# Ordering the mixers' threads by an account of the engines, in place of written latencies

## The chip, the cores and the metric

One core of a Trainium2 chip runs one program. The metric is the device time of one execution in microseconds (us). TensorE (PE) does the matrix products, VectorE (DVE), ScalarE (ACT) and GpSimd (POOL) the rest; SyncE (SP) issues nearly all weight loads. Every engine works through its own queue in program order, so the order in which the program is written down (emitted) is the order in which each engine takes its work up.

## The reference

Two transformer blocks in float32 on 256 tokens of width 1024: three mixers, each followed by a mixture of 32 experts (MoE).

```python
x = first_block(x, c, ...)    # two layers: even mixer, MoE 0, odd mixer, MoE 1
return second_block(x, ...)   # one layer: second mixer, MoE 2, final norm
# even:   o = concat(sliding-window attention, gated linear attention) @ w_out
# odd:    o = block attention (one block of 256 here, 8 heads) @ w_out
# second: o = (gate_nsa * (nsa @ w1) + gate_hg * (hgrn2 @ w2)) @ w_out
# MoE:    two of the 32 experts for each token, silu(t@w1)*(t@w3) @ w2
```

## The kernel before

**Weights.** All weights, some 700 MB, stream once through `ring`, 19 slots of 1 MB. `plan` fills a list in order of use; `pump` (L183 to L195) issues the next load when a slot is free, and `done`/`release` free slots as the program is emitted. SP waits at each load until the slot's last reader has finished.

**Stages.** Even mixer, MoE 0, odd mixer, MoE 1, second mixer, MoE 2. In a MoE each pair of experts takes 12 loads of 1 MB, and PE uses them as they land.

**A mixer** multiplies the activations by its weights in `slab` (from L468): for each 2 x 512 piece of weights `prep` splits the float32 weights in two parts (cast on ACT L461, subtractions on DVE L462 and POOL L463) and PE runs three products. Beside this stream of weight products run smaller threads, all Python generators: in the even mixer `gla` (gated linear attention) and `swa`, `swa_tile` (the window attention, scores at L856, softmax to L871); in the odd mixer `transposed` and eight `head`s (softmax at L1054 to L1063); in the second mixer `nsa_prep`, `nsa_attn` (scores L1269, exponentials L1275, normalisation L1287) and `hgrn` (levels, each ending at L1375). `mix` puts modulation products (`mod`, weights ada_w, the tile condz) between the stream's steps: eight in the even mixer's slabs and two in its first output half, six in the odd mixer, none in the second.

**What sets the order.** `weave` (L213) takes the first thread in its list that is ready, the stream being last, and emits its next step; when none is ready it goes to the one that is ready first. A thread says with `yield (a, b)` that the step took PE a us and that its next step is ready b us after; with `yield (key, ...)` that it waits for flags; `flag(key, lat)` sets a flag to now + lat. All of a, b and lat are written numbers. Those that matter below: each of the four score steps of a `swa_tile` ends with `yield (0.22*nb, 13.3)`; a softmax in `nsa_attn` has 4.0 after the exponentials and 2.0 after the normalisation, and 0.8 after each two score groups; a level of `hgrn` has 7.0 and then 1.0; in the odd mixer's stream the step that reads the gate's rows and issues 15 small loads on ACT's queue (`router` L1614 to L1622 and `second_setup` L1156) ends with `yield (3.8, 0.3)`. The stream waits for the flags of the window attention ("oa") before its first output half in the even mixer, and for "nsa" before its last input slabs in the second.

Of the kernel before, what the change touches and what calls it, by code (L numbers as in the profile page):

```python
# [10 lines left out]
FR = mybir.dt.float32r  # L11
# [108 lines left out]
    return c  # L120


class Net:
    def __init__(self, tc, ctx, A, out):
        self.tc, self.nc, self.A, self.out = tc, tc.nc, A, out
        nc = self.nc
        pool = lambda name, bufs=1, **k: ctx.enter_context(tc.tile_pool(name=name, bufs=bufs, **k))
        c = self.cp = pool("const")
        self.ring = pool("ring", RING)
        self.ps = pool("ps", 8, space=PSUM)  # L130
        self.dp = pool("scratch", space=DRAM)
        self.flip = 0
        self.queue, self.live, self.chunks = [], {}, {}
        self.free, self.reserve, self.wanted = RING, 0, []
        self.now, self.flags = 0.0, {}
        self.more, self.mine, self.extra = [], set(), None
        km = c.tile([P, 476], FT, name="km")
        self.km = km
        self.ident = km[:, 0:128]
        self.ltri = km[:, 128:256]  # L140
        self.ones = km[:, 256:384]
        self.iota = km[:, 384:448]
        self.selc = km[:, 448:464]
        self.tie4 = km[:, 464:468]
        self.tie8 = km[:, 468:476]
        self.x = c.tile([P, NT, D], FT, name="x")
        self.fb = ExitStack()
        self.fp = self.fb.enter_context(tc.tile_pool(name="first", bufs=1, side="right"))
        self.rb = ExitStack()
        self.rp = self.rb.enter_context(tc.tile_pool(name="rows", bufs=1, side="right"))  # L150
        self.ga = self.fp.tile([P, D], FT, name="ga")
        self.ssq = c.tile([P, NT, 4], FT, name="ssq")
        self.mhalf = c.tile([P, 16], FT, name="mhalf")
        nc.gpsimd.memset(self.mhalf, -0.5)
# [52 lines left out]
        self.release(len(keys) - n, reserve)  # L207


    def flag(self, key, lat=0.0):  # L210
        self.flags[key] = self.now + lat

    def weave(self, *gens):  # L213
        th = [[g, self.now, ()] for g in gens]
        while th:
            best = None
            for x in th:
                if any(k not in self.flags for k in x[2]):
                    continue
                r = max([x[1]] + [self.flags[k] for k in x[2]])  # L220
                if r <= self.now + 1e-9:
                    best = (r, x)
                    break
                if best is None or r < best[0]:
                    best = (r, x)
            assert best, [x[2] for x in th]
            r, x = best
            self.now = max(self.now, r)
            try:
                y = next(x[0])  # L230
            except StopIteration:
                th.remove(x)
                continue
            if isinstance(y[0], (int, float)):
                self.now += y[0]
                x[1], x[2] = self.now + y[1], ()
            else:
                x[1], x[2] = self.now, y
        self.flags = {}
# [1777 lines left out]
def body(tc, A, out):  # L2017
    with ExitStack() as ctx:
        ctx.enter_context(tc.manual_schedule())
        n = Net(tc, ctx, A, out)  # L2020
        n.plan_even()
        n.plan_moe(0)
        n.plan_odd()
        n.plan_moe(1)
        n.plan_second()
        n.plan_moe(2)

        n.reserve = 6
        n.even(lambda: n.norm_coeffs(0, 7, 3, 4))
        n.moe(0, n.ev[6], lambda: n.gate_coeffs(0, 5), lambda: n.norm_coeffs(1, 6, 0, 1), 8)  # L2030
        bp = ctx.enter_context(ExitStack())
        n.bias1 = bp.enter_context(tc.tile_pool(name="bias", bufs=1, side="right")).tile([P, 8, T], FT, name="bias1")
        pb = ctx.enter_context(ExitStack())
        n.pre = pb.enter_context(tc.tile_pool(name="pre", bufs=1))
        n.odd(lambda: n.norm_coeffs(1, 7, 3, 4))
        bp.close()
        n.rb.close()
        n.moe(1, n.od[5], lambda: n.gate_coeffs(1, 5), lambda: n.norm_coeffs(1, 8), 14)
        n.fb.close()
        n.second(lambda: n.norm_coeffs(1, 9))  # L2040
        pb.close()
        n.extra = ctx.enter_context(tc.tile_pool(name="extra", bufs=2, side="right"))
        n.more = [n.extra] * 2
        n.moe(2, (), lambda: None, lambda: None, 0)


INPUTS = [
# [23 lines left out]
```

## Time and profile before

| | |
|---|---|
| median of 3 runs (lowest to highest) | 2085.38 us (2081.81 to 2085.57) |
| the profiled execution | 2082.4 us, of which the span of instructions is 2080.6 us |
| PE busy | 1885.0 us, 91% |
| DVE, ACT, POOL busy | 859.2, 431.3, 309.6 us |
| DMA | 725.30 MB, mean 349 GB/s, 421 GB/s in the MoE stages |

The stages, from the span's start: even mixer to about 216 us, MoE 0 to 695, odd mixer to 857, MoE 1 to 1337, second mixer to 1609, MoE 2 to the end. Where the DMA engines are fully busy the loads set the pace; elsewhere one asks what PE waits for.

### The profile page before, as it was taken

To read this page: it belongs to the slowest core of one execution; us is meant where nothing else is said; L and a number is where in the kernel's file an instruction comes from. 1 tells how busy PE (TensorE), PEld (TensorE's weight loads), DVE (VectorE), ACT (ScalarE), POOL (GpSimd) and SP (SyncE) were. 2 spreads that over 40 slices of the span, in tenths; PEclk is the share of its full clock that TensorE was granted. 3 is DMA by queue.
4 is the path that set the end of the run, shared out by engine and by line. 5 is a ranking of instruction groups with operands and counts; after the bars stand their busy time and mean duration, and the time that the engine had idled before them with its cause. 6 is when DMAs were issued, how large, how long until landed. Compare 5 with 4: busy or idle time off the path is not lost. (4 is left out here: it accounts for less than half of the span.)

```text
span 2080.6 us, 25139 instructions
## 1 busy us (share of the span) xinstructions
PE 1885.0 (91%) x10032; PEld 1039.9 (50%) x10032; DVE 859.2 (41%) x1601; ACT 431.3 (21%) x790; POOL 309.6 (15%) x245
## 2 busy tenths in 40 slices
PE   5898899899999889899999999998899999899997
PEld 3656444434444657544343444586788444344443
DVE  3665433323332657633223332367666332222223
ACT  1423211111010333311010111244543111001111
POOL 1331000000000424100000000143443000000000
PEclk8997999999999999999999999899999999999999
DMA  9696999999999966799999999931357999999997
GB/s 322 258 304 236 363 422 422 420 421 421 421 421 406 343 214 247 303 391 421 421 420 421 421 421 421 337 111 41 123 191 270 373 421 421 420 421 421 421 421 270
DMA packets 157542, 725.30 MB, mean 349 GB/s; under 512 B 25305, under 2 KB 43087, under 8 KB 85225
## 3 DMA queue, kind: packets, MB, share of 16 engines
q1 hardware_dynamic: 139216, 716.84, 86.0%
q10 hardware_dynamic: 18201, 6.76, 1.3%
q8 instruction: 82, 1.34, 0.3%
q14 instruction: 43, 0.35, 0.0%
HBM read 722.48 MB, written 1.07 MB: 348 GB/s over the span
## 5 line engine op out<-in xcount | busy, mean ns | idle before, releaser
L258 PE MATMUL ps<-slot,xg 128*64 128x512 f32 x2952 | 680.9, 598 | 0.0
L258 PEld LDWEIGHTS ps<-slot,xg 128*64 128x64 f32 x2952 | 231.0, 138 | 408.7 <-issue 391.7
L258 PE MATMUL ps<-slot,ht 128*64 128x512 f32 (+1 forms) x1592 | 344.8, 574 | 67.6 <-issue 62.9
L258 PE MATMUL ps<-slot 128*128 128x256 f32 (+8 forms) x2230 | 369.9, 326 | 14.0 <-DVE slot L462 9.6
L258 PEld LDWEIGHTS ps<-slot 128*128 128x128 f32 (+3 forms) x2230 | 300.4, 186 | 74.0 <-issue 16.0
L258 PEld LDWEIGHTS ps<-slot,ht 128*64 128x64 f32 x1592 | 130.3, 138 | 257.0 <-issue 244.3
L1908 DVE TENSOR_TENSOR x<-x,ps 128x512 f32<-128x512 f32 x180 | 115.2, 681 | 246.1 <-PE ps L258 246.1
L1882 POOL TENSOR_TENSOR yl<-sg,yh 128x512 fp32r<-128x512 f32 (+1 forms) x68 | 82.4, 1212 | 870.8 <-ACT yh L1881 870.8
L463 POOL TENSOR_TENSOR slot<-slot 128x512 fp32r<-128x512 f32 (+2 forms) x108 | 163.7, 1533 | 282.4 <-ACT slot L461 265.6
L1861 DVE SCALAR_TENSOR_TENSOR hh<-sg,ws,ps 128x512 f32<-128x512 f32 x48 | 53.4, 1113 | 316.5 <-PE ps L258 203.4
L1881 ACT CAST yh<-sg 128x512 fp32r<-128x512 f32 (+1 forms) x68 | 40.3, 593 | 466.1 <-DVE sg L1880 466.1
L462 DVE TENSOR_TENSOR slot<-slot 128x512 fp32r<-128x512 f32 (+2 forms) x108 | 107.4, 1008 | 55.6 <-ACT slot L461 55.1
L1880 DVE TENSOR_TENSOR sg<-ps,ga 128x512 f32<-128x512 f32 (+1 forms) x68 | 44.9, 660 | 178.7 <-PE ps L258 178.7
L258 PEld LDWEIGHTS ps<-u,slot 128*128 128x128 f32 x864 | 104.4, 192 | 23.4 <-issue 17.0
L461 ACT CAST slot<-slot 128x1024 fp32r<-128x1024 f32 (+2 forms) x108 | 106.5, 1020 | 44.8 <-PE ps L258 24.7
L258 PE MATMUL ps<-u,slot 128*128 128x256 f32 (+1 forms) x864 | 109.7, 285 | 3.5 <-DVEq L1743 3.5
L1857 ACT ACTIVATE sg<-ps 128x512 f32<-128x512 f32 x48 | 28.7, 598 | 297.9 <-PE ps L258 297.9
L258 PE MATMUL ps<-yh,pg 128*128 128x512 f32 (+1 forms) x204 | 87.2, 429 | 0.7 <-ACT yh L1881 0.7
L258 PE MATMUL ps<-yl,pg 128*128 128x512 f32 (+1 forms) x204 | 78.5, 387 | 4.3 <-POOL yl L1882 4.0
L399 ACT ACTIVATE xg<-ps,cf 128x256 f32<-128x256 f32 (+1 forms) x72 | 38.9, 540 | 168.0 <-PE ps L258 168.0
L1933 POOL TENSOR_TENSOR slot<-x,rows 128x512 f32<-128x512 f32 x2 | 2.5, 1270 | 463.0 <-DVE x L1929 463.0
L1884 ACT CAST yh<-ps 128x512 fp32r<-128x512 f32 (+1 forms) x34 | 19.0, 560 | 222.7 <-PE ps L258 222.6
(333 smaller groups left out, 1569.3 us busy)
## 6 DMA issues: line engine op xcount, KB each, us to landing
slot<-moe_w SPq DMA_DIRECT2D x376, 1024.0 KB, 17.7
slot<-w_gate SPq DMA_DIRECT2D x59, 1024.0 KB, 19.7
slot<-w_down SPq DMA_DIRECT2D x55, 1024.0 KB, 18.5
slot<-w_up SPq DMA_DIRECT2D x54, 1024.0 KB, 18.8
slot<-ada_w SPq DMA_DIRECT2D x48, 1024.0 KB, 8.8
slot<-w_in SPq DMA_DIRECT2D x20, 1024.0 KB, 5.7
slot<-odd_w_in SPq DMA_DIRECT2D x12, 1024.0 KB, 16.8
more<-w_up SPq DMA_DIRECT2D x10, 1024.0 KB, 16.1
```

The costliest lines, as they stand in the source:

```text
L258: self.nc.tensor.matmul(out, lhsT=lhsT, rhs=rhs, start=start, stop=stop)
L399: self.nc.scalar.activation(out, p, AF.Identity, scale=a, bias=nb[:, k:k + 1])
L461: nc.scalar.copy(wh, src)
L462: nc.vector.tensor_sub(wl[:, 0], src[:, 0], wh[:, 0].bitcast(FT))
L463: nc.gpsimd.tensor_sub(wl[:, 1], src[:, 1], wh[:, 1].bitcast(FT))
L1857: nc.scalar.activation(sg, ps, AF.Silu)
L1861: nc.vector.scalar_tensor_tensor(ha.rearrange("s k p -> s p k"), st["sg", p].rearrange("s (p k) -> s p k", k=4), st["ws", p], ps.rearrange ...
L1880: nc.vector.tensor_mul(y, ps, self.ga[:, sl])
L1881: nc.scalar.copy(yh, y)
L1882: nc.gpsimd.tensor_sub(yl, y, yh.bitcast(FT))
L1884: nc.scalar.copy(yh, ps)
L1908: nc.vector.tensor_add(self.x[:, t, sl], self.x[:, t, sl], ps)
```

## The change

The written numbers stay in the code but are hardly used. An object `Queues` is told of every instruction as the program is built. It keeps a clock for each engine (its queue's end), the times at which pieces of tiles are written and read, and one clock for all loads (400 bytes a ns, 2.0 us to land; an issue takes its engine 0.4 us). `now` is its clock of PE. A step whose b is 0 leaves the thread ready at once, as before; a step whose b is not 0 makes it ready when the last result of that step, by the account, is there. A flag is set to the end of its step's results so far. Results of loads issued by ACT count in this; those of SP don't. No instruction is added to the program or taken out.

```diff
+class Queues:
+    def cost(self, kind, engine, ins, outs):
+        n = max([o[5] for o in outs], default=1)
+        if engine == "PE":
+            if kind != "InstMatmult":
+                return 0.05
+            one = len(ins) and ins[0][6] == FR
+            width = outs[0][2] - outs[0][1]
+            t = n * 0.000417 * (1 if one else 2 if n <= 128 else 4) + 0.013
+            return t * (0.55 if width <= 64 else 1.0)
+        base, slope = {"Activation": (0.2, 0.00082), "DVE": (0.16, 0.00104), "Pool": (0.4, 0.0023)}.get(engine, (0.05, 0.0))
+        return base + slope * n
+
+    def __call__(self, inst):
...
+        start = max(self.clock.get(engine, 0.0), self.clock.get("PE", 0.0) if dma else 0.0)
...
+        if dma:
+            size = sum(128 * o[5] * 4 for o in outs)
+            self.clock[engine] = start + 0.4
+            end = max(start, self.clock.get("fetch", 0.0)) + size / 4e5
+            self.clock["fetch"] = end
+            end += 2.0
+        else:
+            end = start + self.cost(kind, engine, ins, outs)
+            self.clock[engine] = end
+            if outs:
+                end += 0.06
...
+        if outs and not (dma and engine == "SP"):
+            self.end, self.touched = max(self.end, end), True
...
+    @property
+    def now(self):
+        return self.queues.clock.get("PE", 0.0)
+
     def flag(self, key, lat=0.0):
-        self.flags[key] = self.now + lat
+        self.flags[key] = max(self.now, self.queues.end) if self.queues.touched else self.now
...
             r, x = best
-            self.now = max(self.now, r)
+            q.clock["PE"] = max(self.now, r)
+            q.end, q.touched = 0.0, False
...
             if isinstance(y[0], (int, float)):
-                self.now += y[0]
-                x[1], x[2] = self.now + y[1], ()
+                x[2] = ()
+                x[1] = self.now if not y[1] else max(self.now, q.end) if q.touched else self.now + y[1]
```

## Rows read from the trace of the kernel before

**Rows 1.** The page: busy us, share and instructions; DMA busy in 40 slices.
```profile
PE 1885.0 (91%) x10032; PEld 1039.9 (50%) x10032; DVE 859.2 (41%) x1601; ACT 431.3 (21%) x790; POOL 309.6 (15%) x245
DMA  9696999999999966799999999931357999999997
```
**Rows 2.** Windows: length, busy PE, PEld, DVE, ACT, POOL, granted clock, DMA share, GB/s.
```profile
45.00:151.70 106.70, 97.76 (x581) 65.90 (x581) 70.76 (x125) 37.05 (x52) 40.24 (x32) 0.97 0.84 292
151.70:176.10 24.40, 12.77 (x50) 7.43 (x48) 14.23 (x46) 12.00 (x41) 1.55 (x1) 0.65 0.76 283
240.00:695.00 455.00, 418.35 (x2046) 188.00 (x2044) 140.02 (x220) 53.87 (x102) 43.25 (x37) 0.99 1.01 414
752.00:776.00 24.00, 17.66 (x93) 10.95 (x92) 6.74 (x17) 6.97 (x14) 4.72 (x3) 0.86 0.73 240
1392.00:1488.00 96.00, 81.55 (x606) 66.03 (x606) 69.35 (x178) 47.58 (x110) 30.92 (x22) 0.93 0.24 77
1488.00:1609.00 121.00, 119.40 (x924) 109.13 (x923) 80.51 (x116) 57.88 (x80) 52.16 (x34) 0.99 0.57 204
1650.00:2040.00 390.00, 361.33 (x1752) 158.14 (x1749) 110.65 (x188) 36.89 (x68) 0.00 (x0) 1.00 1.01 421
```
**Rows 3.** Waits of PE, 240 to 690: us in total, times, longest.
```profile
PE ps L258 <- issue: 21.0, 14, 1.6
```
**Rows 4.** Waits of PE in the even mixer, 45 to 216.
```profile
PE ps L268 <- DVE slot L871: 6.6, 1, 6.6
...
PE ps L268 <- DVE slot L798: 3.9, 1, 3.9
```
**Rows 5.** Timeline, even mixer: start us, us, instruction, [idle before <- releaser].
```profile
108.63 0.92 PE L258 MATMUL ps<-kT,qT 64*128 64x256 f32 x8
...
151.04 0.70 PE L258 MATMUL ps<-kT,qT 64*128 64x256 f32 x4
...
164.49 2.22 PE L268 MATMUL ps<-km,slot 128*128 128x128 f32 x8 [6.57 <-DVE slot L871]
```
**Rows 6.** The same on DVE: eight normalisations of one window-attention tile.
```profile
163.99 2.19 DVE L871 TENSOR_SCALAR slot<-slot,den 128x256 f32<-128x256 f32 x8
```
**Rows 7.** Timeline of ACT's queue in the odd mixer, first and last of 15 issues.
```profile
754.17 0.58 ACTq L1619 DMA_DIRECT2D wr<-moe_w_group  x1
...
761.87 0.35 ACTq L1156 DMA_DIRECT2D ll<-hg_lb_logits  x1
762.26 0.92 ACT L254 CAST slot<-ps 128x256 fp32r<-128x256 f32 x3 [7.51 <-DMA k_cmp<-k_cmp]
```
**Rows 8.** Timeline of PE at the same place.
```profile
759.47 1.92 PE L258 MATMUL ps<-slot,condz 128*32 128x512 f32 x16
761.32 3.06 PE L258 MATMUL ps<-slot 128*128 128x512 f32 x12
770.67 0.88 PE L268 MATMUL ps<-km,sc 128*128 128x128 f32 x3 [6.29 <-DVE sc L1063]
```
**Rows 9.** Waits of PE in the second mixer, 1337 to 1609.
```profile
PE ps L268 <- DVE slot L1287: 13.3, 9, 2.5
```
**Rows 10.** Timeline of PE, second mixer: two score steps, the last slab before "nsa".
```profile
1436.34 1.13 PE L258 MATMUL ps<-kd,qT 64*128 64x256 f32 x8
...
1438.99 1.14 PE L258 MATMUL ps<-kd,qT 64*128 64x256 f32 x8
...
1465.05 8.34 PE L258 MATMUL ps<-slot 128*128 128x512 f32 x36
1475.85 0.33 PE L268 MATMUL ps<-km,slot 128*128 128x128 f32 x1 [2.46 <-DVE slot L1287]
```
**Rows 11.** Timeline of DVE: the last reduction of the first of these score steps.
```profile
1438.33 0.42 DVE L1269 CUSTOM_DVE_ANT_0 slot<-ps,k_causal 128x256 f32<-128x256 f32 x1
```
**Rows 12.** Two lines of the kernel: count, ns min/median/max, first to last start.
```profile
L1287 DVE TENSOR_SCALAR slot<-slot,den x32: 273/340/1347, 1405.8 to 1480.1; 128x128 f32<-128x128 f32 x16, 128x256 f32<-128x256 f32 x16
...
L1375 DVE COPY_PREDICATED slot<-lvm,ps x7: 724/736/754, 1433.3 to 1516.8; 128x512 f32<-128x512 uint32 x7
```

More of the change, by code (lines that the diff above doesn't have):

```diff
@@ L120, in host_constants, with __init__, part @@
     return c
+class Queues:
+    def __init__(self):
+        self.clock, self.tiles, self.end, self.touched = {}, {}, 0.0, False
+    @staticmethod
+    def part(arg):
+        ap = getattr(arg, "bass_ap", None)
+        if ap is None or not hasattr(ap, "tensor"):
+            return None
+        try:
+            dims, off = [(int(a), int(b)) for a, b in ap.ap], int(ap.offset)
+        except (TypeError, ValueError):
+            return None
+        step = max(1, dims[0][0])
+        lo = off % step
+        hi = lo + sum(abs(a) * (b - 1) for a, b in dims[1:]) + 1
+        n = 1
+        for a, b in dims[1:]:
+            n *= b
+        return ap.tensor.name, off // step, off // step + dims[0][1], lo, hi, n, arg.dtype
+    def cost(self, kind, engine, ins, outs):
[10 more added lines that the diff above has]
+    def __call__(self, inst):
+        engine = str(inst.engine).split(".")[-1]
+        kind = type(inst).__name__
+        outs = [p for p in map(self.part, inst.outs) if p]
+        ins = [p for p in map(self.part, inst.ins) if p]
+        dma = "DMA" in kind
+        start = max(self.clock.get(engine, 0.0), self.clock.get("PE", 0.0) if dma else 0.0)
+        for parts, write in ((ins, False), (outs, True)):
+            for p in parts:
+                for q in self.tiles.get(p[0], ()):
+                    if (write or q[5]) and q[0] < p[2] and p[1] < q[1] and q[2] < p[4] and p[3] < q[3]:
+                        start = max(start, q[4] + (0.07 if q[6] != engine else 0.0))
+        if dma:
[9 more added lines that the diff above has]
+                end += 0.06
+        for parts, write in ((ins, False), (outs, True)):
+            for p in parts:
+                seen = self.tiles.setdefault(p[0], [])
+                seen.append((p[1], p[2], p[3], p[4], end, write, engine))
+                if len(seen) > 96:
+                    del seen[:32]
+        if outs and not (dma and engine == "SP"):
+            self.end, self.touched = max(self.end, end), True
@@ L134, in __init__ @@
         self.free, self.reserve, self.wanted = RING, 0, []
-        self.now, self.flags = 0.0, {}
+        self.flags, self.queues = {}, Queues()
+        nc.push_inst_callback(self.queues)
         self.more, self.mine, self.extra = [], set(), None
@@ L207, in done @@
         self.release(len(keys) - n, reserve)
+    @property
+    def now(self):
+        return self.queues.clock.get("PE", 0.0)
     def flag(self, key, lat=0.0):
-        self.flags[key] = self.now + lat
+        self.flags[key] = max(self.now, self.queues.end) if self.queues.touched else self.now
     def weave(self, *gens):
         th = [[g, self.now, ()] for g in gens]
+        q = self.queues
         while th:
@@ L2044, in body @@
         n.moe(2, (), lambda: None, lambda: None, 0)
+        n.nc.pop_inst_callback()
 INPUTS = [
```

## The prediction

> **What bounds the kernel now.** I read the page first: PE is busy 91% of the span, and the slices of DMA alternate between long full stretches and dips [rows 1]. The windows say which stretch has which limit [rows 2]. In the MoE stages the DMA share is 1.01 while PE still has room (418.35 of 455.00 us in MoE 0, 361.33 of 390.00 in MoE 2), and the waits of PE there are short ones that no engine ends, 14 of up to 1.6 us [rows 3]: the loads set the pace. In the mixers it is the other way round: DMA share 0.84, 0.76, 0.73, 0.24 in four stretches, PE nearly full where nothing goes wrong (119.40 of 121.00 us at the end of the second mixer) and short of work elsewhere [rows 2]. So a MoE ends a fixed time after its loads have become continuous, and that moment hangs on when the mixer before it gives up its slots. A microsecond taken from the PE path of a mixer moves the loads of the following MoE by about a microsecond and comes out at the end; idle time inside a MoE is not touched by the change at all.
>
> The whole prize is therefore PE's idle time inside the three mixers. There are three places, and they differ in what could fill them.
>
> **Even mixer, the tail.** From 151.70 to 176.10 PE is busy for 12.77 of 24.40 us, at a mean granted clock of 0.65 [rows 2]. The waits are for the window attention and the gated attention: 6.6 us for the normalisation at L871, 3.9 us for L798 [rows 4]. The stream has emitted all it may and stands at the "oa" flags. Why is the window attention so late? Its score steps: one at 108.63, PE work 0.92 us for both tiles, the last ones only from 151.04 on [rows 5]. They are spaced by the written 13.3 us each. Under the account a score step is ready again when its own reductions are done: by the constants in the diff about 0.9 us of PE and 0.43 us for each of two reductions of 256 columns, say 3 us with what stands in DVE's queue and one stream step. Four steps then take some 12 us in place of over 42, so the attention ends some 30 us earlier in the queue, near 146, before the stream reaches its wait. The tail then holds only its work. What is that at the full clock? The mean of 0.65 between the levels 1.2 and 2.4 GHz means 17.1 us at the lower; 11.6 us of the 24.4 were idle; the busy part at full clock is then between 6.4 us (all 12.77 at the lower level) and 10.0 us (all idle time at the lower level); I take 8. Gain at most 24.4 - 8 = 16.4 us. Cover: the attention's 8 us move among slab steps that PE has to do anyway, and DVE was busy 70.76 of 106.70 us there [rows 2], so it has room for the moved 14.23 us, but not without queueing. The change also brings an error of its own: eight modulation products are priced 8 x (512 x 0.000417 x 4 + 0.013) x 0.55 = 3.8 us by the account, while the trace has 1.92 us [rows 8]. After each of them the account's PE clock is 1.9 us ahead and a thread's next step can come that much too early. Ten of them: between 0 and 19 us; since a loss needs a thread becoming ready just there, I take 3. Even mixer: **-13 us** (from -16.4 to +3: nothing gained and that loss kept).
>
> **Odd mixer, the loads issued by ACT.** ACT issues 15 small loads between 754.17 and 762.22 and computes nothing [rows 7]; the head whose transposes are at PE's front waits 6.29 us at 770.67 [rows 8]. The account does see the issues (15 x 0.4 = 6 us, against 8.05 in the trace), so a head's step after them is put back. But the stream's step ends with b = 0.3, and its new meaning is "when the last result is there", and landed loads of ACT count: 6 us of issues, some 1.5 us of copies and 2.0 us to land hold the stream for about 9.5 us in place of 0.3. What stood in front of the head's transposes from 759.47 on, one modulation and 12 products (1.92 + 3.06 = 5.0 us), goes behind it. The new wait is then 6.3 + 5.0 less what the head gains where no weight split stands before its normalisation on DVE. That gain I bound by 0 and 5.0 us and take 4. With 2 us from other early transposes in this mixer I put the odd mixer at **0 us** (-6.3, the wait gone, to +5.0). Behind the held stream stand its weight splits on ACT and DVE and so the slots for SP; the heads gain from that, the loads lose as much as the stream.
>
> **Second mixer, the softmaxes.** From 1392 to 1488 PE is idle for 14.45 us [rows 2], 13.3 us of it at transposes that wait for the normalisation at L1287 [rows 9]. The written 4.0 + 2.0 us are too short. The account puts the transposes later, and slab steps go before them. But that alone wins nothing: the stream's last slab before "nsa" ends at 1473.4, before the last of the attention's waits at 1475.85 [rows 10]. Had the slabs filled the earlier gaps, they would have run out sooner, and PE would have waited at the end. Filling pays only with work that would otherwise come after 1488, and `hgrn` has that: its seven levels end from 1433.3 to 1516.8, 83.5/6 = 13.9 us apart [rows 12], where the account will bring a level every 6 to 7 us (one POOL subtraction of 1.6 us, an exponential of 1.0, four DVE operations of 0.7, by its constants). I credit 8 of the 14.45 us. Against it: a score step is now followed only after its reductions. The second one of rows 10 came 2.65 us after the first; the last reduction of the first ended at 1438.75 [rows 11], 2.41 us after its start, so with a slab step's grain the next comes 0 to 1.5 us later than now. Four such places: 0 to 6, I take 3. And DVE, which carries the chain, gets `hgrn`'s levels ahead of it: I take 2 here; the case where it is much more is a rival. Second mixer: 8 - 3 - 2, **-3 us** (-14.45 to +28).
>
> What the account prices wrongly on DVE can be seen in one row: the 32 normalisations took 273 ns at the least and 1347 at the most [rows 12], and eight of them 2.19 us where POOL is quiet [rows 6]; the account gives each of 256 columns 426 ns always, 3.4 us for eight. The Trainium skill, SBUF — State Buffer, section "SBUF: two separate sides", says that such a DVE operation and one of GpSimd exclude each other for the whole of an instruction. The maximum in this trace agrees with that. By that rule the levels' POOL subtractions, brought closer together, speak against this change; a whole subtraction by the account's own price (1.6 us) in each of the four softmaxes would take 6 us off the gain.
>
> The sum: -13 + 0 - 3 = -16 us. Against the profiled execution's own 2082.4 us (span 2080.6 and 1.8 around it) that is 2066.4; this execution lies 3.0 us under the median of the runs shown, so on the median's scale it is 2085.4 - 16 = **2069.4 us**. Instructions, weight bytes and MoE stages cost nothing more or less.
>
> **Rivals.**
>
> *The gap only moves* (2085). The even tail closes, but what is moved forward crowds DVE in 105 to 150, and the odd and second mixer lose 13 us between them (the bounds +5.0 and +28 leave room). Speaks for it: each of the three mixers has a stretch where PE waits for a chain and not for its own queue. Against: the even tail is plain want of work, and the four mean DMA shares show slots and loads waiting, not full.
>
> *The levels overtake the attention* (2100, slower). In the second mixer `hgrn` runs at its natural pace. Two levels fall into each of the four softmaxes, and their DVE work goes into the queue ahead of the normalisations: 2 x 4 x 0.74 = 5.9 us, and two normalisations each at 1.35 in place of 0.27 us, 2.1 us [rows 12]: 8 us x 4 = 32. PE has 4 us more of `hgrn`'s products to fill with. So "nsa" comes late and the mixer loses 28 us; with the even mixer's gain 2085.4 + 28 - 13 = 2100. It decides from the point where the four softmaxes lose over 4 + 13 + 4 = 21 us together, 5 us each. For it: DVE was busy already 69.35 of 96.00 us. Against: that leaves 26.65 us of room, and `nsa_attn` goes before `hgrn` when both are ready.
>
> *Everything closes* (2048). The even tail by 16.4, the odd wait by 6.3, the second mixer's 14.45 filled with `hgrn`: 2085.4 - 37.
>
> That the change doesn't alter the order is hardly possible: 13.3 against some 3 us is too far apart. If it were so the time would be 2085, and it is counted with the moved gap.
>
> **How the numbers follow.** Forecast 0.50 with its own range of 2058 to 2081 (even -13 by 4, second -3 by 6, odd 0 by 4, added roughly); moved gap 0.17; levels overtake, or another loss of that size in an order that nobody has looked at, 0.24; all closes 0.09. For 8 in 10 the range reaches from 2048 to 2102. A measurement of this kernel can tell some 0.2%, 4.2 us, from no change: faster is 0.47 of the forecast and 0.09, 0.56; same is the rest of the forecast and most of the moved gap, 0.17; slower 0.27.
>
> **What the changed profile would show.** Even: the last kT,qT products of the window attention before 130, no idle PE of over 2 us ahead of the first output half, and granted clock near 1.0 there; if "oa" still ends a wait of several us, the first step is wrong. MoE: stretches of the same length, each beginning earlier; if the mixer ends earlier and the MoE does not, the loads didn't move and my main assumption falls. Odd: a wait of 6 to 9 us after ACT's 15 issues; gone means I misread the held stream. Second: L1375 closer than 10 us apart, fewer waits for L1287; if instead the stretch from the first L1287 to the first Sigmoid slab after "nsa" grows by over 10 us, the levels overtook. The prediction is wrong altogether if PE finds new waits of tens of us, above all for loads or weight splits that the account believes to be there.

## The result, and the profile after

The change makes the kernel slower: 2111.82 us median (2109.05 to 2120.6, 4 runs) against 2085.48 (2081.81 to 2087.46, 4 runs) beside it, a ratio of 1.0136 [1.0102 to 1.0169]. I had forecast 2069.4 in a range of 2048 to 2102; the time lies above the range. The profiled execution of the kernel after is its slowest, 2120.6 us (span 2118.8), 8.8 over its median; so sizes of the loss are taken below from ratios, and the traces show the places. The page after, the lines that answer to [rows 1]:

```profile
PE 1902.8 (90%) x10032; PEld 1049.3 (50%) x10032; DVE 851.4 (40%) x1601; ACT 432.5 (20%) x790; POOL 308.0 (15%) x245
...
DMA  8668999999999847799999999931256899999997
```

The number of instructions is the same on every engine. The windows of the kernel after (length, busy PE, PEld, DVE, ACT, POOL, granted clock, DMA share, GB/s), to be held against [rows 2]; the last two are the softmax attention of the second mixer and what follows it:

```profile
45.00:151.70 106.70, 86.92 (x489) 57.93 (x490) 61.57 (x138) 40.77 (x83) 28.98 (x23) 0.88 0.65 234
151.70:188.50 36.80, 32.11 (x175) 19.60 (x174) 20.75 (x36) 9.27 (x13) 14.28 (x11) 0.95 1.03 361
240.00:695.00 455.00, 419.58 (x2048) 186.39 (x2046) 137.94 (x217) 49.53 (x90) 40.49 (x33) 0.99 1.01 413
...
1414.80:1524.60 109.80, 84.28 (x645) 67.62 (x646) 73.53 (x187) 53.73 (x114) 31.63 (x23) 0.88 0.19 65
1524.60:1657.90 133.30, 128.18 (x917) 114.67 (x915) 78.37 (x140) 53.75 (x79) 50.07 (x32) 0.99 0.61 223
```

MoE 0 is as it was. The even mixer's hole has moved: the first stretch, nearly full before (97.76 of 106.70 us), now has 19.8 us without work, and the tail is filled but for one wait. Stage by stage (a mixer ends, and a MoE begins, with the routing's first product of `top`; a mixer begins with its first product of `sel,x`; read from the timelines of PE):

| us | even | MoE 0 | odd | MoE 1 | second | MoE 2 |
|---|---|---|---|---|---|---|
| before | 227.7 | 467.4 | 173.9 | 468.1 | 284.3 | 459.1 |
| after | 234.1 | 468.4 | 187.9 | 470.2 | 297.3 | 460.8 |
| of it PE at the lower clock, before and after | 41.0, 47.8 | 10.2, 10.2 | 17.1, 31.2 | 10.2, 16.5 | 27.3, 37.7 | 9.3, 13.7 |

All three mixers are longer. The even one varies between executions in one and the same order: in the twelve traces that have it in the written order it takes 222.3 to 227.7 us, and in the other trace with the order of the kernel after (`e1_even`) 231.3.

**Even mixer.** PE's waits after, from 45 us to the routing (us in total, times, longest), in place of [rows 4]:

```profile
PE ps L334 <- issue: 8.0, 1, 8.0
PE ps L344 <- DVE qs L898: 5.6, 1, 5.6
PE ps L344 <- DVE slot L874: 4.7, 1, 4.7
PE ps L344 <- DVE rows L406: 1.9, 1, 1.9
```

The wait for the window attention's normalisation is gone, as forecast, but three others stand ahead of it. The longest is in the timeline of PE, and what points to its cause is in those of ACT's and SP's queues:

```profile
59.09 1.13 PE L334 MATMUL ps<-ab,gup 16*128 16x256 f32 x4
68.18 2.04 PE L334 MATMUL ps<-slot,fl 128*128 128x512 f32 x2 [7.96 <-issue]
```
```profile
53.56 0.39 ACTq L681 DMA_DIRECT2D slot<-bvec  x1
```
```profile
82.02 2.04 SPq L264 DMA_DIRECT2D slot<-ada_w  x3
```

The first thing that PE does at 68.18 is `bias_tile`'s flip of the 1 MB bias table that ACT began to load at 53.56, 14.6 us earlier. Its written wait was 23.4 us (`yield (0.0, 23.4)`); the account reckons about 5 with no other load ahead of it (1 MB at 400 bytes a ns, and 2.0 us). Everything queued behind it on PE waits too, the slots stay taken, and SP's next weight load is issued only at 82.02. The row says `issue` and names no load; that the load ends the wait is shown below, where the wait goes when loads no longer count.

**Odd mixer.** ACT's queue after, first and last of the same 15 issues as in [rows 7], and PE there, as in [rows 8]:

```profile
771.45 0.57 ACTq L1695 DMA_DIRECT2D wr<-moe_w_group  x1
...
779.14 0.37 ACTq L1232 DMA_DIRECT2D ll<-hg_lb_logits  x1
779.54 0.65 ACT L330 CAST slot<-ps 128x256 fp32r<-128x256 f32 x2 [7.52 <-DMA k_cmp<-k_cmp]
```
```profile
774.12 0.82 PE L334 MATMUL ps<-slot 128*128 128x128 f32 x4
780.63 1.65 PE L334 MATMUL ps<-pT,slot 128*128 128x128 f32 x6 [5.68 <-ACT pT L325]
```

The stream is held, the products that stood in front are gone, and PE waits 5.68 us where it waited 6.29. The other waits of this mixer are new or longer; the last of them is its own bias step, again ahead of its load:

```profile
PE ps L334 <- ACT pT L325: 5.7, 1, 5.7
PE ps L344 <- DVE qk L707: 4.7, 6, 1.9
PE ps L334 <- DMA bias<-bvec: 3.5, 1, 3.5
```

**Second mixer.** Waits there, in place of [rows 9], and the longest of them on PE and ACT:

```profile
PE ps L344 <- DVE slot L1363: 17.4, 7, 11.3
PE ps L334 <- DVE mx L1345: 4.2, 2, 2.4
```
```profile
1493.77 1.13 PE L334 MATMUL ps<-kd,qT 64*128 64x256 f32 x8
1494.99 2.75 PE L334 MATMUL ps<-slot 128*64 128x64 f32 x38
1497.67 1.13 PE L334 MATMUL ps<-kd,qT 64*128 64x256 f32 x8
...
1514.99 2.26 PE L344 MATMUL ps<-km,slot 128*128 128x128 f32 x5 [11.29 <-DVE slot L1363]
```
```profile
1501.39 1.28 ACT L1461 ACT_TABLE_LOAD   x1 [3.01 <-DVE slot L1460]
1502.68 1.06 ACT L1461 ACTIVATE slot<-slot 128x1024 f32<-128x1024 f32 x1
1503.76 1.28 ACT L1614 ACT_TABLE_LOAD   x1
1505.05 0.60 ACT L1614 ACTIVATE slot<-ps 128x512 f32<-128x512 f32 x1
1505.67 1.28 ACT L1351 ACT_TABLE_LOAD   x1
1506.96 0.51 ACT L1351 ACTIVATE slot<-slot,mx 128x256 f32<-128x256 f32 x1
```

Two groups of score products (kd,qT) end in one maximum (`mx`), and only then do the exponentials L1351 begin. Between the groups stand a step of the levels (32 products) and 6 slab products, 3.90 us from start to start. In the same softmax of the kernel before it was the step of the levels alone, 2.15 us:

```profile
1460.34 1.13 PE L258 MATMUL ps<-kd,qT 64*128 64x256 f32 x8
1461.41 1.15 PE L258 MATMUL ps<-slot 128*64 128x64 f32 x32
1462.49 1.13 PE L258 MATMUL ps<-kd,qT 64*128 64x256 f32 x8
```

Over the four softmaxes these distances add up to 18.8 us in place of 9.6. In the last one, besides, ACT takes an exponential of the levels and a Silu of the stream in front of the exponentials, with three table loads. From its first reduction to its first exponential (1506.96) it takes 12.5 us:

```profile
1494.50 0.42 DVE L1345 CUSTOM_DVE_ANT_0 slot<-ps,k_causal 128x256 f32<-128x256 f32 x1 [1.48 <-PE ps L334]
```

### The profile page after: what moved, and what is told of

Read it like the earlier page. It is cut to its first block, busy times and chain, and to the rows that moved or that the text cites. A ratio compares the mean times of both kernels' runs of the same rounds, so it can differ in the third digit from the quotient of the medians.

```text
span 2118.8 us, 25138 instructions
## 1 busy us (share of the span) xinstructions
PE 1902.8 (90%) x10032; PEld 1049.3 (50%) x10032; DVE 851.4 (40%) x1601; ACT 432.5 (20%) x790; POOL 308.0 (15%) x245
## 5 line engine op out<-in xcount | busy, mean ns | idle before, releaser
L538 DVE TENSOR_TENSOR slot<-slot 128x512 fp32r<-128x512 f32 (+2 forms) x108 | 97.7, 913 | 60.0 <-ACT slot L537 59.0
L537 ACT CAST slot<-slot 128x1024 fp32r<-128x1024 f32 (+2 forms) x108 | 107.3, 1020 | 47.8 <-PE ps L334 29.7
L334 PEld LDWEIGHTS ps<-u,slot 128*128 128x128 f32 x864 | 104.1, 192 | 23.4 <-issue 17.0
L1933 ACT ACTIVATE sg<-ps 128x512 f32<-128x512 f32 x48 | 28.7, 598 | 300.2 <-PE ps L334 300.2
## 6 DMA issues: line engine op xcount, KB each, us to landing
slot<-w_gate SPq DMA_DIRECT2D x59, 1024.0 KB, 19.3
```

Of the source, the lines that this page charges most:

```text
L334: self.nc.tensor.matmul(out, lhsT=lhsT, rhs=rhs, start=start, stop=stop)
L537: nc.scalar.copy(wh, src)
L538: nc.vector.tensor_sub(wl[:, 0], src[:, 0], wh[:, 0].bitcast(FT))
L1933: nc.scalar.activation(sg, ps, AF.Silu)
```

## The experiments

Each was timed beside the kernel before on the same chip (its median there 2081 to 2086 us), so the ratios are what is compared; with 2085 us, 0.1% is 2.1 us.

### Which mixer loses

The account orders one mixer and the written latencies the other two; `account` is set ahead of each `weave`, and PE's order in that mixer is that of the kernel after.

```diff
     def now(self):
-        return self.queues.clock.get("PE", 0.0)
+        return self.queues.clock.get("PE", 0.0) if self.account else self.written
...
-            if isinstance(y[0], (int, float)):
+            if isinstance(y[0], (int, float)) and not self.account:
+                self.written += y[0]
+                x[1], x[2] = self.written + y[1], ()
```

> The account sets the order in the even mixer alone; the odd and the second mixer keep the written latencies. Theory (each loss stands where its idle time stands in the trace of the changed kernel, and the losses add): the even mixer ends some 6 us later than before, so 2085 + 6 = 2091 us. Rival (a late even mixer shifts all loads and what follows suffers too, or the loss is none of the mixers' own): 2085 or over 2100.

> The account in the odd mixer alone. Theory: between the trace of before and that of the changed kernel the odd mixer grows by some 14 us, so 2085 + 10 to 15 = 2095 to 2100 us. Rival (the growth is a consequence of the late even mixer before it): within 4 us of 2085.

> The account in the second mixer alone. Theory: the second mixer grows by 13 us of its own, so 2095 to 2098 us. Rival (a consequence of what came before): within 4 us of 2085.

Measured: even 2088.67, 1.0018 [1.0008 to 1.0028]; odd 2089.09, 1.0033 [1.0019 to 1.0046]; second 2095.64, 1.0049 [1.0029 to 1.0068]. All three lose, the second most, though its interval meets that of the odd one; together 1.0%, some 21 us, of the 1.36% [1.02 to 1.69]. The intervals meet; whether the rest is more than their width stays open. For the odd mixer the theory had 10 to 15 us and missed: it loses about 7, and takes 182.8 us in its trace where it takes 187.9 in the kernel after. So some 5 of the 14 us of the stage table are absent when the even mixer before it keeps its written order.

### The loads that count as results

```diff
-        if outs and not (dma and engine == "SP"):
+        if outs and not dma:
```

In all three mixers, and then (`e9_even`) in the even mixer alone, the others by written latencies:

> The changed kernel, in which no load counts as a step's result (SP's didn't, now ACT's don't either): a step that only loads keeps its written latency, 23.4 us for the bias, and the odd mixer's stream isn't held for 15 small loads. Theory (the bias products at PE's front before their load has landed, 7.96 and 3.50 us of idle PE and the lower clock after them, and the held stream, 5.68 us, make up most of what the even and the odd mixer lost): 2112 - 20 = 2092 us. Rival (the order of the rest costs the time, the second mixer above all): 2105 to 2112 us.

> The account orders the even mixer alone, and results of loads issued by ACT don't count in it, so that the bias step keeps its written 23.4 us. Theory: the loss of the account in the even mixer alone (2088.7, some 4 us) is the bias step's wait for a load that has not landed; then PE does not wait for 8 us near 68 and the time is 2081 to 2085, below the kernel before by up to 4 us, the closed tail's share. Rival: the loss is the early transposes of the window attention (gaps of 5.6 and 1.9 us near 100), which stay; then 2087 to 2090.

Measured: 2095.15, 1.0037 [1.0017 to 1.0056], in place of 1.0136; in its profiled execution, the slowest of five (2104.22), the even mixer takes 225.9 us (after 234.1), the odd one 178.1 (187.9). The even mixer alone: 2085.36, 0.9997 [0.9984 to 1.0011]. The wait of 8.0 us is gone from its trace. So the account's loss in the even mixer is the bias step, as far as two ratios can tell whose intervals just meet. What remains when it is gone is no gain that the runs can tell from nothing. PE's waits in `e9_even`, from 45 us to the routing:

```profile
PE ps L354 <- DVE qs L908: 7.0, 2, 6.1
PE ps L354 <- DVE slot L884: 4.7, 1, 4.7
PE ps L354 <- DVE rows L416: 1.9, 1, 1.9
```

The last score products (kT,qT) end at 105.8 us (before: after 157), the tail is closed up to one wait of 4.7 us for `gla`'s gating. But the transposes for the window attention's first scores now come before their operands: 6.1 and 1.9 us. All idle time of PE in this mixer after the first weight product is 21.1 us against 23.3 before.

### The window attention's spacing by itself

The kernel before, one number changed:

```diff
-                yield (0.22 * nb, 13.3)
+                yield (0.22 * nb, 2.0)
```

> The kernel before with one number changed: the score steps of the window attention end with 2.0 in place of 13.3 us. Theory (the prediction's step for the even mixer: the tail from 151.7 to 176.1 is the attention's spacing and nothing else): the tail closes and the time falls by 10 to 16 us, 2070 to 2075. Rival (the attention moved forward crowds DVE and PE's waits come up earlier in the mixer, as in the changed kernel, whose window attention is early and whose even mixer is not shorter even where the bias is no wait): within 4 us of 2084.

Measured: 2091.52, 1.0027 [1.0012 to 1.0043], slower. PE's waits, from 45 us to the routing:

```profile
PE ps L258 <- DVE slot L251: 5.6, 1, 5.6
...
PE ps L258 <- DVE pT L251: 4.9, 1, 4.9
PE ps L268 <- DVE slot L798: 2.8, 1, 2.8
```

The 6.6 us at L871 are gone, and copies out of PSUM (L251) that now queue behind the attention's reductions take 5.6 and 4.9. Two ways of closing the tail, and neither gains.

### The second mixer: levels, tables, attention

The account in the second mixer alone; a thread in `kept` keeps its written numbers.

```diff
-                x[1] = self.now if not y[1] else max(self.now, q.end) if q.touched else self.now + y[1]
+                x[1] = self.now + y[1] if not y[1] or x[0] in self.kept else max(self.now, q.end) if q.touched else self.now + y[1]
```

> The account in the second mixer alone, but the hgrn thread keeps its written latencies. Theory (the levels overtake the attention: with the account alone the second mixer was 13 us longer): the loss falls to 2 to 4 us, 2086 to 2088. Rival (the attention's own spacing and ACT's order cost the time): 2093 to 2097 as with the whole account.

> The account orders the second mixer alone, and within it the softmax attention keeps its written latencies (4.0 and 2.0 us); the levels of the recurrence go by the account. Levels theory: what costs the second mixer is that the levels' exponentials and DVE work come more closely, in front of the softmaxes; then this is as slow as the account in the whole second mixer, 2093 to 2097, and the stretch from the first product with kr,qT to the last pcT grows to 105 us or more from 95.4. Rival, the attention's own steps: each waits for all its results and then for stream steps put in between, which lengthens the chain; then this stands at 2084 to 2088, and the loss left when the levels kept their numbers (some 4 us) was the attention's. If both carry half, 2089 to 2091.

Levels kept: 2089.32, 1.0027 [1.0017 to 1.0037], between the two theories. Attention kept: 2104.54, 1.0094 [1.0080 to 1.0109], slower than with both threads under the account (1.0049) and than either theory had it. Nor is it the mechanism of the levels theory: the attention's chain got shorter (table below), and the recurrence fell behind it, so that 160.2 us follow the chain in place of 133.5.

To price the tables, the stream's Silu in `s_hg` becomes an Exp, which leaves the order as it was and computes another gate: in the account's second mixer, in the kernel before, and with the levels kept.

```diff
-                nc.scalar.activation(gs[:, t], p, AF.Silu)
+                nc.scalar.activation(gs[:, t], p, AF.Exp)
```

> The account in the second mixer alone, instruction for instruction in the same order, but the gate of hgrn takes an exponential in place of Silu (another result), so that ACT keeps its function table where the two Silu stand between exponentials. Theory (the 11.29 us of idle PE come from three table loads of 1.28 us each just ahead of the last softmax, which the account does not price, and from what waits behind them): the idle time falls to some 7 us and the time to 2090 to 2092. Rival (the softmax is late because the levels' exponential and a weight split stand ahead of it, whatever the tables): within 2 us of 2095.6.

> The kernel before with the same exponential in place of Silu (another result), to tell what the missing table loads are worth by themselves. Both theories: 0 to 3 us faster than before, 2081 to 2084.

> The account in the second mixer alone, hgrn with its written latencies and the exponential in place of Silu (another result). Theory (two causes that add: the levels' pace and the table loads between Silu and exponentials, each worth about half of the 12 us): 2084 to 2087 us. Rival (one cause seen twice, the exponentials of the levels beside the two Silu: either cure takes the same half away): 2089 to 2090 us.

Measured: 2089.91, 1.0024 [1.0014 to 1.0034]; in the kernel before 2086.38, 1.0002 [0.9992 to 1.0012]; with the levels kept 2090.4, 1.0026 [1.0016 to 1.0036]. The tables cost nothing before and about half of the loss under the account, but the two remedies don't add, as the rival had it: half of the loss is in neither.

### The score groups

What is common to all of these shows when the four softmaxes are set side by side (from the first reduction L1269 to the first exponential L1275, both as numbered before; chain: first product of kr,qT to the end of the last of pcT; lower clock: PE in the whole second mixer):

| us | to the first exponential, four softmaxes | sum | chain | lower clock | mixer |
|---|---|---|---|---|---|
| before | 3.5, 6.9, 6.3, 3.9 | 20.6 | 95.4 | 27.3 | 284.3 |
| after | 4.3, 8.2, 8.8, 12.5 | 33.8 | 109.8 | 37.7 | 297.3 |
| levels kept (e4_second_hgrn) | 4.8, 8.2, 8.0, 8.0 | 29.0 | 105.2 | 34.1 | 290.7 |
| Silu to Exp (e5_second_silu) | 4.6, 8.2, 8.8, 8.3 | 30.0 | 102.2 | 30.7 | 289.7 |
| attention kept (e9_attn) | 3.3, 4.4, 3.9, 8.9 | 20.5 | 89.9 | 47.8 | 304.2 |
| e10_scores | 2.5, 2.1, 3.1, 3.1 | 10.8 | 91.5 | 58.2 | 297.2 |
| e10_before_scores | 5.1, 12.9, 9.6, 8.1 | 35.6 | 111.3 | 47.8 | 302.9 |
| e11_copy | 2.3, 2.1, 3.1, 3.1 | 10.6 | 92.1 | 34.1 | 286.6 |

The expectation of `e10_scores` misreads two of these: it has 5.0 for the 6.9 before and 11.1 for the 12.5 after.

A score step ends with `yield (0.43 * nb, 0.8)`. Since 0.8 is not 0, the account holds the thread until the reductions are done, and whatever is ready goes between the two groups of one maximum. Two experiments take that apart: the account in the second mixer with this step ready at once, and the kernel before with 2.0 in place of 0.8.

```diff
-                        yield (0.43 * nb, 0.8)
+                        yield (0.43 * nb, 0.0)
```
```diff
-                        yield (0.43 * nb, 0.8)
+                        yield (0.43 * nb, 2.0)
```

> The account orders the second mixer alone, and only there the score step of the softmax attention is ready again at once (its second number 0.8 becomes 0.0, which the account takes as ready). Score theory: what lengthens the attention's chain by 14 us is that the two score groups of each softmax are torn apart (from the first reduction of a softmax to its first exponential 4.3, 8.2, 8.9 and 11.1 us, against 3.5, 5.0, 6.3 and 3.9 before); then these four fall back to some 4 to 6 us each, the chain to 96 to 101 us from 109.8, and the time is 2084 to 2089 against 2095.6. Rival, the levels' work on ACT and DVE: the four intervals stay over 7 us in the later softmaxes and the time stays at 2092 to 2097.

> The kernel before, with its written latencies, and one number changed: a score step of the softmax attention is ready again after 2.0 us in place of 0.8, so that stream steps come between the two score groups of a softmax. Score theory: the four intervals grow by 2 to 5 us each, the chain from 95.4 to 103 or more, and the time is 2089 to 2095. Rival: the spacing does nothing by itself, 2083 to 2088.

The second is clear: 2096.87, 1.0077 [1.0064 to 1.0090]. One number, and the kernel before loses more than the account lost in the whole mixer, with intervals grown in the same way. The first was a miss in time, and its mechanism came as described: intervals and chain fell, further than the theory said, and PE's idle time in the mixer went from 31.2 to 19.3 us, below the 20.1 of before. Yet PE's busy time there rose from 266.1 to 277.9 us, and the time is 2096.2, 1.0073 [1.0060 to 1.0086].

### Where that gain went: the clock

The windows of `e10_scores` from 1480 to 1540, and PE's timeline:

```profile
1480.00:1540.00 60.00, 55.57 (x411) 44.20 (x410) 29.46 (x44) 17.05 (x25) 13.58 (x10) 0.74 0.29 101
```
```profile
1500.19 1.06 PE L354 MATMUL ps<-km,slot 128*128 128x128 f32 x8
1503.73 31.67 PE L344 MATMUL ps<-slot 64*128 64x128 f32 x128 [2.47 <-ACT slot L335]
```

The recurrence's transposes end at 1501.26, PE waits 2.47 us for ACT's copies of them, and from 1503.70 the granted clock is 0.5, 1.2 GHz, for 30.72 us, though PE then works without a break. The products are the recurrence's last ones, 80 of 128 columns that use half the array's rows, half its columns or both, with slab products between; the clock comes back at 1534.42, 3.8 us after the last of them. In the kernel before the same run from the first of them to the last took 17.6 us (1523.82 to 1541.43) at the full clock, with 42 slab products in it; here it takes 26.9 us with 24. In the kernel before the idle time ahead of them was 0.24 us:

```profile
1523.82 2.06 PE L258 MATMUL ps<-slot 64*128 64x128 f32 x14 [0.24 <-ACT slot L249]
```

The last experiment gives the second transpose a wait that the account fills with 12 slab products (and, in the odd mixer, has the 11 setup loads issued by SP, the edit of the next section):

```diff
-            yield (0.9, 0.0 if t == 0 else 0.0)
+            yield (0.9, 0.0 if t == 0 else 1.0)
```

> As the account in the second mixer with score steps ready at once, and one more number: after its second transpose the recurrence is ready again only when the copies on ACT are done (0.0 becomes 1.0), so that 12 slab products stand between the transposes and the products that read the copies. Besides, the 11 setup loads of the odd mixer are issued by SP (-9 us, as measured alone). Clock theory: with the score groups together the chain is 91.5 us, but the second mixer stays at 297 us because after an idle 2.5 us on these copies (at 1503.7) the granted clock is 0.5 for 30.7 us, through products that the kernel before runs at full clock; without the idle time the clock stays up, the mixer takes 280 to 286 us and the time is 2070 to 2078. Rival: the small products of the recurrence, brought together, keep the clock low themselves; then the mixer stays at 292 to 298 us and the time is 2083 to 2089.

Measured: 2073.96, 0.9954 [0.9941 to 0.9966]. The same views:

```profile
1480.00:1540.00 60.00, 55.46 (x486) 49.57 (x481) 33.88 (x46) 24.71 (x36) 22.70 (x15) 0.97 0.41 141
```
```profile
1494.90 1.68 PE L344 MATMUL ps<-slot 128*128 128x256 f32 x12
1497.61 17.08 PE L344 MATMUL ps<-slot 64*128 64x128 f32 x116 [1.03 <-ACT slot L335]
```

PE is busy for the same 55.5 us of the 60 and gets 75 more products done. The idle time ahead is 1.03 us, the clock stays up, and the mixer takes 286.6 us in place of 297.2. PE's idle time in the whole mixer is the same (19.6 against 19.3 us), its busy time 10.9 us less, its time at the lower clock 24.1 us less. So the clock carried the missing 10 us. Ahead of these products the two orders differ only in the 12 slab products put into the idle time; whether the idle time or the want of these products brings the clock down is not separated.

Two more rows bear on it. In `e7_priced` (below) PE waits 5.31 us in the even mixer ahead of 64-row and 64-column products, and the granted clock is 0.5 for 30.72 us there too. In `e11_copy` itself a wait of 2.27 us, ahead of products on the whole array, is followed by only 3.41 us at the lower clock:

```profile
150.93 3.78 PE L349 MATMUL ps<-slot 64*128 64x256 f32 x12 [5.31 <-DVE slot L342]
```
```profile
1521.27 0.86 PE L354 MATMUL ps<-km,slot 128*128 128x128 f32 x4 [2.27 <-DVE slot L1537]
```

In the twenty traces three stretches at the lower clock last 30.72 us: those of `e10_scores` and `e7_priced`, and one over the same products of the recurrence in `e10_mended`. No other is longer than 17.1 us. This speaks for what follows the idle time, and not for its length alone; no run changes one without the other.

That the account has a part in the 0.9954 is not shown. The SP loads alone give 0.9965 [0.9951 to 0.9979] (next section), the intervals overlap, and the second mixer takes 286.6 us against 284.3 before.

### ACT's issues, and corrected prices

The kernel before, with the 11 loads of `second_setup` issued by SP:

```diff
-            nc.scalar.dma_start(self.S[nm], src)
+            nc.sync.dma_start(self.S[nm], src)
```

> The kernel before, in which the 11 loads of second_setup are issued by SP and not by ACT. Theory (the 6.29 us of idle PE at 770.67 in the odd mixer, and the lower clock after it, are ACT's 8 us of issuing): 2085 - 4 to 8 us, 2077 to 2081. Rival (SP's own loads, queued behind these, or the weight splits on DVE end the wait as late): within 3 us of 2085.

> The same with the 11 small setup loads of the odd mixer issued by SP in place of ACT. The two edits lie in different mixers, so the gain of the second (2076.6 against 2085.5, 9 us) should add: 2072 to 2076 by the theory, 2078 to 2081 by the rival. If the account in the even mixer is worth something, this is the fastest kernel of the case.

Measured: 2076.57, 0.9965 [0.9951 to 0.9979], faster than both kernels. PE's wait of [rows 8], after the same 12 products:

```profile
761.47 3.06 PE L258 MATMUL ps<-slot 128*128 128x512 f32 x12
766.11 0.61 PE L268 MATMUL ps<-km,sc 128*128 128x128 f32 x3 [1.58 <-DVE sc L1063]
```

6.29 us have become 1.58, and the odd mixer takes 167.3 us in place of 173.9. With the even mixer of `e9_even` besides: 2076.47, 0.9962 [0.9947 to 0.9977], nothing more.

The account itself can be made truer: ACT's loads out of the results, modulation products at half the price, 1.28 us for a change of table, GpSimd's power by its columns, and DVE waiting for GpSimd.

```diff
-            return t * (0.55 if width <= 64 else 1.0)
+            return t * (0.275 if width <= 32 else 0.55 if width <= 64 else 1.0)
...
+            self.table = func
+            return 1.283
...
+            return min(1.07, max(0.0, self.clock.get("Pool", 0.0) - start))
```

> The changed kernel with an account that knows what the traces show: no load counts as a result, the modulation products at half their old price, 1.283 us for a change of ACT's function table, 0.13 us a column for GpSimd's small powers, and a DVE operation on tiles in SBUF that waits for a running GpSimd operation, 1.07 us at most. Theory (the loss is the account's prices; with them right the rule is at least as good as the written latencies): 2080 to 2088 us. Rival (the rule itself: each thread is emitted as soon as its inputs are there, so that the small threads' bursts on DVE and ACT stand ahead of weight splits and of each other): 2090 us or more, as with the loads alone taken out (2095).

Measured: 2113.29, 1.0145 [1.0128 to 1.0162], as slow as with the wrong prices, but by other stages. The odd mixer is mended (175.2 us after 187.9), the even one is worse (245.3 after 234.1) by the stretch almost wholly at the lower clock that was named above:

```profile
148.00:180.00 32.00, 28.34 (x94) 15.71 (x95) 10.76 (x26) 4.29 (x7) 1.01 (x1) 0.52 0.37 109
```

and the second stays at 300.2. Last, the account in all mixers with three edits: loads not counted, score steps ready at once, setup loads by SP.

> The account in all three mixers with three edits: results of loads issued by ACT don't count, the score step of the softmax attention is ready again at once, and the 11 setup loads of the odd mixer are issued by SP. If the three losses have been named rightly, what is left against the kernel before is small: even 0, odd -9 plus the 4 us of its early transposes, second 0 to 4: 2080 to 2086. If the account costs in places not named yet, over 2090.

Measured: 2096.87, 1.0063 [1.0049 to 1.0077], a miss: even 225.6, odd 174.6, second 297.5 us with 58.3 at the lower clock: the clock again, as in `e10_scores`. Its six executions go the same way: the two with a mean granted clock of 0.970 take 2089.19 and 2090.45 us, the other four, at 0.963 to 0.967, 2095.54 to 2100.93. In the odd mixer the account still costs 7.3 us against `e8_setup_sp`'s 167.3; what is left there are eight waits for the transposes' operands (`qk`), 6.1 us together.

## Why the prediction was wrong

**The carry** held. MoE stages are 1 to 2 us longer, and what a mixer loses comes out at the end; idle time inside a MoE was not touched.

**Even mixer, -13 forecast, +4 measured (1.0018).** Two steps failed. First, "the even tail is plain want of work": the attention's steps did move some 44 us forward, its last scores end at 113.5 us, where I had said before 130. But `e9_even` and `e3_swa` show that the idle time then lies elsewhere, ahead of transposes that wait for DVE or of copies behind DVE's reductions. The cover that I named, slab steps and a DVE with 36 us of room, was an average over a stretch; the steps need DVE at one moment. That is the mechanism of my rival *the gap only moves*, to which I gave 0.17; its 2085 had no price for the bias step. Second, the bias step. I had written that results of ACT's loads count and worked it out for the odd mixer alone; the same rule takes 23.4 us down to about 5 for a load that takes over 14. The sentence on loads that the account believes to be there was the general case of it, without a term in the sum.

**Odd mixer, 0 forecast, about +7 measured (1.0033).** The held stream came as described, with a wait of 5.68 us for the forecast 6 to 9, and counting the loads costs about 4.7 us (the odd mixer takes 182.8 us in `e1_odd` and 178.1 in `e2_no_loads`, one execution each; against the 187.9 of the kernel after it is 9.8). Part of it is a wait for the bias load, 2.5 us in `e1_odd`, which had no term. What I mis-sized is "2 us from other early transposes": 178.1 against 173.9 is 4.2, and with ACT's issues out of the way it is 7.3. Nor does the paragraph add up to its 0: a wait of 6.3 + 5.0 - 4 = 7.3 us in place of 6.3, and the 2 us as a cost, make a loss of 3.

**Second mixer, -3 forecast, about +10 measured (1.0049).** The failing step is the term for the score steps, "four such places: 0 to 6, I take 3". I asked how late the second score step would come, 0 to 1.5 us each, and counted on stream steps as its grain; it came 2.3 us later on average (18.8 - 9.6 = 9.2 us in four), and ACT's order ahead of the last exponentials added to it. The intervals to the exponentials grew by 33.8 - 20.6 = 13.2 us, the chain by 14.4, the mixer by 13.0. `e10_before_scores` shows the same loss, 15.0, 15.9 and 18.6, from that spacing alone. The credit of 8 us failed with it: the levels came 11.6 us apart (before 13.9), not 6 to 7, and PE's idle time over the attention's chain rose from 14.45 to 25.5 us.

**The rival that the levels overtake** had the right sign and a place nearby, 2100 with a chance of 0.24, and is not what happened in the form that I gave it. Its price was DVE work of the levels ahead of the normalisations. With the levels under the account and the attention not (`e9_attn`) the chain is shorter than before, 89.9 us. What stands ahead is a step between the two score groups and, in the last softmax, table loads on ACT: in that one, Silu to Exp brings 12.5 down to 8.3 us, and the levels' written pace brings it to 8.0. The Trainium skill, ScalarE: Activation LUTs, section "What ACT_TABLE_LOAD costs", gives 1283 ns for the load and 1380 ns more for a drain; the trace agrees with the first (1.28) and shows no room for the second: the load at 1503.76 starts 0.02 us after the activation before it ends, and the next activation starts 1.29 us after the load.

Of the signs that I had named for this mixer, the waits for L1287 became fewer, 7 in place of 9, but grew from 13.3 to 17.4 us, L1375 did not come closer than 10 us, and the stretch up to the end of "nsa" did grow by over 10 us; I would have read that as the levels' doing, and the table of the score groups says otherwise.

**The account's price errors**, to which I gave 3 us, are not the whole cause: with five of them corrected the kernel is as slow, the odd mixer better and the even one worse. I put it down to the rule, each step as soon as its own results are there: it has no notion that two groups feed one maximum, that a thread ahead takes work from later, or that a short idle time can cost clock. That no truer account would do better is not shown.

**The clock** has no term in the second mixer's part of my sum. `e10_scores` shows that it can outweigh all idle time won back.

## What to carry to other kernels

An order by earliest readiness serves the queues and not the chain: keep together what feeds one reduction, and price the wait that a step puts on the thread it interrupts, not only on its own. When a written latency is replaced by a computed one, list every step whose written number was long for a reason (here 23.4 us for a load), and reckon each anew. Judge a closed gap by the length of its stage and the granted clock in it, for idle time that goes may come back as time at the lower clock.

## What was not expected of the hardware

- One idle stretch of 2.47 us, ahead of products on half the array's rows or columns, was followed by 30.72 us at 1.2 GHz with PE busy throughout; with 12 slab products there and 1.03 us idle there was no drop. The price is some 10 us. After 2.27 us ahead of products on the whole array it was 3.41 us.
- Small loads cost the engine that issues them: 15 issues on ACT take 8.05 us [rows 7]. Given to SP, 11 of them no longer delay ACT's exponentials, and the kernel is 0.35% faster.
